# A two-layer hybrid decoder trunk: the first stage rebuilt with packed vectors, single-column modulation products and 28 instead of 16 filler products

## The chip, the cores and the metric

The kernel runs on one core of a Trainium2 chip. The metric is the device time of one execution in microseconds (us); lower is better. Three runs of the kernel before gave 257.09, 257.39 and 258.31 us, median 257.39.

The names of the engines: PE is TensorE (its matmuls), PEld its weight loads, DVE is VectorE, ACT is ScalarE, POOL is GpSimd, SP is SyncE, which issues nearly all DMAs.

## What is computed

The input x is 256 x 1024 (one batch), c is a conditioning vector of 1024. Two layers, each `x <- x + gate(c) * mixer(RMSNorm(x) * (1 + scale(c)) + shift(c))`. The first stage, which the change touches, is this part of the reference:

```python
cs = jax.nn.silu(c)
shift, scale, gate = jnp.split(cs @ mod_w[layer] + mod_b[layer], 3, axis=-1)
h = _modulate(_rmsnorm(x, norm_g[layer]), shift, scale)
...
u, g = jnp.split(h @ w_in, 2, axis=-1)
```

After it come a causal convolution of width 4, the RG-LRU gates and scan, an output projection, then shared keys and values, an attention layer with its own projections, and a last RMSNorm. All arrays are f32. The large products are done as three products each (`hi*hi`, `lo*hi`, `hi*lo`) of operands that are split into a rounded part `_hi` and a rest `_lo`.

## The kernel before

The 1024 features are 8 tiles of 128 (`KT`), the 256 positions 2 tiles (`ST`). All weights arrive in blocks of 512 KB, in the order of the string `ORDER`, over SP's queue, into 11 raw buffers (`NRAW`); a block's buffer is free again when its last reader is done. The host packs the blocks (`packed`, L105); it does not change a number.

Nothing is issued as it is written. Each operation is recorded (`Plan.record`, L154), and `Plan.order` (L362) sets an order for every engine with a table of costs, 80 random trials and priorities; the copies, the splits and the scalings (`plan.copy`, `plan.affine`, `plan.scale`) go to ACT or to DVE as it decides. The result is a fixed order on each engine: an instruction waits for all that stand ahead of it on its engine. Because one line issues all recorded operations, nearly every instruction has the line L409 (or L169, those that the planner gave an engine).

The first stage, by the names that the trace shows:

- SP loads c as 8 rows of 128, x in three pieces (`xr`), mod_b and norm_g as rows (`pa`), then the blocks. POOL loads seven more small vectors as rows (`pb`).
- PE runs filler products of `ones` (`warm`, L530: 16 there, and 4 in the bank `ga` ahead of the first real product). Each 128x128 f32 product is two records in the trace.
- silu(c) is made on the 8 rows, turned by a PE transpose (`pt_c`) and spread to 32 equal columns (`csB`); `pa` and `pb` are turned by PE too (`pt_a`, `pt_b`) and copied to `paT`, `pbT` by DVE.
- RMSNorm of x: squares and root on ACT (`sq_a`, `rv_a`), the rest on DVE (`rn`, `ry`, `rt`), the scaled rows `xn_a`, then 16 PE transposes (`tp_a`) and four copies to `xnT`.
- Shift and scale of layer 0: for the tiles 0 and 1 `mod_one` (L719), which is 16 products with 32 equal columns of csB as the stationary operand, four of them side by side in the array (`gvm0s`: 32 records), a copy (`partm0s`), one product with `sel2` that sums the four strips and turns the result (`mc_m0s`: 2 records) and two DVE operations (`sg4m0s`). The tiles 2 and 3 and the tiles 4 and 5 go in pairs with 256 columns (`mod_pair`, L642: `gvm`, `partm`, `mc_m`), the tiles 6 and 7 are summed on DVE (`mod_sum`).
- `mod_apply` (L725) makes `hrm`, `h_hi`, `h_lo` of a tile, and `u_rows` (L783) and `pair_T` (L506) do the three-part products `u` and `ga` with the split weights `wu`, `wga`. Each is one record a part.

Then `pj_wgc` (L498), the gates `pa` and `px` (L880), ACT's chain of exponentials and square roots, `r_wo`, a second RMSNorm (`rms("b...")`), `v`, `k`, and the attention layer.

Of the kernel before, what the change touches and what calls it, by code (L numbers as in the profile page):

```python
# [10 lines left out]
F32 = mybir.dt.float32  # L11
# [7 lines left out]
P = 128  # L19
# [6 lines left out]
NEG = -1e30  # L26
NRAW = 11
NSPL = 4
NWARM = 16
NWARM2 = 4  # L30
SUM0 = 3
LEAD = 2
CUT = 384

ORDER = """
    s0 wu0 s1 wu1 wga0 m01 wu2 wu3 m02 wga1 wu4 wu5 m03 wga2 wu6 wu7 wga3 wgc0 gax0 gax2 gax3 g0-0
    gax1 wgc1 g0-1 wo0 mk0 mk1 wo1 mk4 mk2 mk3 mk5 wv0 mk7 mk6 wv1 wv2 wv3 m10 wka0 wka1 wv4 wv5
    wka2 m12 wv6 m11 wv7 m13 m15 wka3 m14 wkb0 m16 m17 wkb1 wgb0 wgb1 wqa0 wgb2 wgb3 wqa1 wgb4 wgb5
    wqa2 wgb6 wgb7 wqa3 wqb0 wqb1 g1-0 wp0 wp1 g1-1
"""  # L40
# [7 lines left out]
def blocks():  # L48
# [4 lines left out]
    def want(name, shape, *src):  # L53
        out.append((name, shape, src))
# [8 lines left out]
    for b in ORDER.split():  # L63
        nm, i = b[:-1], int(b[-1])
        if nm == "s":
            for x, c0 in (("h", 0), ("c", D)):
                want(f"m0{x}0_{i}", (KT, P), ("mod_w", 0, 0, D, c0 + i * P, P))
        elif nm == "m0" and i >= SUM0:
            for q in range(4):
# [30 lines left out]


BLOCKS = blocks()


# [15 lines left out]
class Plan:  # L120
# [164 lines left out]


    def _forward(self, urge):
        ops, succ = self.ops, self.succ
# [11 lines left out]
        while len(seq) < n:  # L300
# [43 lines left out]
            for j in succ[i]:  # L344
                if ops[j]["pre"][i]:
                    at[j] = max(at[j], fin[i] + (950 if o["fn"] == "dma_start" else self._lat(o, ops[j])))
# [81 lines left out]
@with_exitstack  # L428
def kernel(ctx: ExitStack, tc: tile.TileContext, x, c, mod_b, norm_g, rg_conv_w, rg_conv_b,
                       rg_b_a, rg_b_x, rg_lambda, kv_norm_g, kv_mod_b, final_norm_g, pack, out):  # L430

# [14 lines left out]

    x, c, out = x[0], c[0], out[0]

# [11 lines left out]

    def split_into(raw, hi, lo):
        plan.copy(hi, raw)
        V.tensor_sub(lo, raw, hi.bitcast(F32))


    def wsplit(name):
        while len(halves) <= windex[name]:
            n = weights[len(halves)]
            t = got[n]
            shape = list(t.shape)  # L470
            hi = splp.tile(shape, F32R, tag="whi", name=n + "_hi", bufs=NSPL)
            lo = splp.tile(shape, F32R, tag="wlo", name=n + "_lo", bufs=NSPL)
            split_into(t, hi, lo)
            halves[n] = hi, lo
        return halves[name]
# [43 lines left out]
    pa = const.tile([64, P], F32, name="pa")  # L519
    SP.dma_start(pa[0:48], mod_b.rearrange("l (k p) -> (l k) p", p=P))  # L520
    SP.dma_start(pa[48:64], norm_g.rearrange("l (k p) -> (l k) p", p=P))
    load_all()
# [50 lines left out]

    def rms(nm, parts, early=None):
        bias, nbias = eps, neps
        for i, row in enumerate(parts):
            w = row.shape[-1]
            sq = tmp.tile([P, w], F32, tag="xn" if w > 512 else "tg", name=f"sq_{nm}{i}")
# [19 lines left out]

    def norm_T(row, rstd, xnT, s, nm):
        xn = tmp.tile([P, D], F32, tag="xn", name="xn_" + nm, bufs=2)  # L600
        plan.scale(xn, row, rstd)
        for q in range(2):
            ps = pbank(f"tp_{nm}{q}")
            for k in range(4):
                PE.transpose(ps[:, k * P:(k + 1) * P], xn[:, (4 * q + k) * P:(4 * q + k + 1) * P], ident)
            plan.copy(xnT[:, 4 * q:4 * q + 4, s * P:(s + 1) * P], ps.rearrange("p (k n) -> p k n", n=P))


# [19 lines left out]
    def mod_cols(tag, n, quads, gain, bias, pbank=pbank):  # L628
        gv = pbank(f"gv{tag}")
        gemv(gv, n * P, quads)  # L630
        part = tmp.tile([P, n * P], F32, tag="part", name=f"part{tag}", bufs=3)
        plan.copy(part, gv[:, 0:n * P])
# [85 lines left out]

    def mod_one(nm, i, k, gain, bias, pbank=pbank):  # L719
        ch = [got[f"{nm}{w}{i}_{k}"] for w in "hc"]  # L720
        quads = [[(csB[:, kt], ch[q // 2][:, kt]) for kt in range(q % 2, KT, 2)] for q in range(4)]
        m = 2 * i + k
        return mod_cols(f"{nm}s{m}", 1, quads, gain[:, m:m + 1], bias[:, m:m + 1], pbank)

# [29 lines left out]
    warm(NWARM, pbank("warm"))  # L754
    pt = bank("pt_a")
    PE.transpose(pt[:, 0:64], pa, ident[0:64, 0:64])
    paT = const.tile([P, 64], F32, name="paT")
    V.tensor_copy(paT, pt[:, 0:64])
    modbT = paT[:, 0:48].rearrange("p (l w k) -> p l w k", l=2, w=3)
# [11 lines left out]

    m0s = [mod_one("m0", 0, 0, *args0, bank)]
    for s in range(ST):
        norm_T(xr[:, s], rms(f"a{s}", [xr[:, s, 0:512], xr[:, s, 512:]] if s else [xr[:, s]], None if s else th[:, 0:1]), xnT, s, f"a{s}")
    m0s.append(mod_one("m0", 0, 1, *args0))

# [9 lines left out]

    for k in range(2):
        mod_apply("m0", k, 1, m0s[k], xnT, h0_h, h0_l)
        u_rows(k)
    nxt = mod_pair("m0", 1, *args0)  # L790
    pair_T(gb, "wga", h0_h, h0_l, 0)

    pt = pbank("pt_b")
    PE.transpose(pt[:, 0:88], pb, ident[0:88, 0:88])
    pbT = const.tile([P, 88], F32, name="pbT")
    V.tensor_copy(pbT, pt[:, 0:88])
    cwT = pbT[:, 0:32].rearrange("p (j k) -> p j k", j=4)
# [8 lines left out]


    nl = const.tile([P, KT], F32, name="nl")
    V.tensor_scalar(nl, lamT, -1.0, None, ALU.mult)
    na = const.tile([P, KT], F32, name="na")  # L810
    V.tensor_tensor(na, lamT, nl, ALU.min)
# [19 lines left out]

    for i in range(1, 4):
        mod_apply("m0", 2 * i, 2, nxt, xnT, h0_h, h0_l)
        if i < 3:
            nxt = (mod_pair if i + 1 < SUM0 else mod_sum)("m0", i + 1, *args0)
        for kt in (2 * i, 2 * i + 1):
            u_rows(kt)
        pair_T(gb, "wga", h0_h, h0_l, i)
# [247 lines left out]
    def fin(s, sl, b):  # L1086
# [26 lines left out]

_INS = ['x', 'c', 'mod_b', 'norm_g', 'rg_conv_w', 'rg_conv_b', 'rg_b_a', 'rg_b_x', 'rg_lambda',
        'kv_norm_g', 'kv_mod_b', 'final_norm_g', 'pack']
_OUTS = [((1, 256, 1024), 'float32')]
# [26 lines left out]
```

## Time and profile before

| | |
|---|---|
| median of three runs | 257.39 us (257.09 to 258.31) |
| the profiled execution | 257.7 us, of which 255.7 us from the first to the last instruction |
| PE busy | 242.2 us (95%), 1823 matmul records |
| weight loads (PEld) | 215.7 us (84%) |
| DVE, ACT, POOL busy | 208.8, 161.2, 18.3 us |
| DMA | 72.24 MB, mean 283 GB/s |
| granted TensorE clock | 0.992 of full speed (mean) |

The 2.0 us between 257.7 and 255.7 lie outside the instructions. "Busy" of PE says little here, since it is nearly always busy; what matters is when its first real product starts, what stands ahead of it, and in which stretches PE is the engine that ends last.

### The profile page before, as it was taken

What the parts mean: (1) busy time and instruction counts of PE and PEld (TensorE: products, weight loads), DVE (VectorE), ACT (ScalarE), POOL (GpSimd) and SP (SyncE); (2) the same over time, 40 slices, a digit from 0 to 9 for tenths busy, and PEclk for the clock granted to TensorE, in tenths of its full rate; (3) what the DMA queues carried; (4) which work ended last, traced back from release to release, by engine and by line L of the source; (5) the groups of instructions that cost most, each with busy time, mean ns of one, the idle gap of its engine ahead of it and who ended that gap; (6) DMA issues with size and microseconds to landing.
All of it is one profiled execution on the core that took longest, in us unless ns stands there. A gap on an engine that the chain in (4) does not pass through costs nothing.

```text
span 255.7 us, 4865 instructions
## 1 busy us (share of the span) xinstructions
PE 242.2 (95%) x1823; PEld 215.7 (84%) x1823; DVE 208.8 (82%) x378; ACT 161.2 (63%) x288; POOL 18.3 (7%) x31
## 2 busy tenths in 40 slices
PE   8899999999999996997999999999999999999970
PEld 7697799999897874865898898999999998889870
DVE  2773799899969999999898999973766789798483
ACT  7662755595799995079943385863537365786242
POOL 8100000000000033000000000010000000005030
PEclk9999999999999999999999999999999999999996
DMA  6999999992697879999999999986897520000003
GB/s 214 410 417 420 413 420 417 420 415 91 238 352 314 309 270 360 419 396 383 420 316 378 395 393 415 416 299 261 253 354 292 173 82 3 1 0 3 1 17 147
DMA packets 20695, 72.24 MB, mean 283 GB/s; under 512 B 2728, under 2 KB 3008, under 8 KB 20672
## 3 DMA queue, kind: packets, MB, share of 16 engines
q1 hardware_dynamic: 19840, 71.15, 71.9%
q0 software_dynamic: 688, 0.59, 0.9%
q8 instruction: 14, 0.23, 0.4%
q10 hardware_dynamic: 144, 0.20, 0.2%
q14 instruction: 9, 0.07, 0.1%
HBM read 70.87 MB, written 1.05 MB: 281 GB/s over the span
## 4 chain that ended last, share of the span: by engine, by line
PE 77%; ACT 12%; DVE 7%; issue 2%; DVEq 0%; ACTq 0%
PE u L409 9%; PE g L409 9%; PE v L409 9%; PE r_wp L409 6%; PE ga L409 5%; PE pj_wkb L409 5%; PE pj_wqb L409 5%; PE q L409 5%; PE k L409 4%; PE r_wo L409 3%; DVE x L409 3%; PE sc L409 3%; ACT L409 3%; PE warm L409 2%; PE pj_wgc L409 2%
## 5 line engine op out<-in xcount | busy, mean ns | idle before, releaser
L409 ACT ACT_TABLE_LOAD x14 | 18.0, 1283 | 1.0 <-PEq L1126 0.7
L409 PE MATMUL u<-h_lo,wu_hi 128*128 128x256 f32 x64 | 18.1, 285 | 0.0
L409 PE MATMUL u<-h_hi,wu_lo 128*128 128x256 f32 x64 | 18.1, 284 | 0.0
L409 PE MATMUL g<-h_hi,wgb_hi 128*128 128x256 f32 x64 | 18.0, 283 | 0.0
L409 PE MATMUL g<-h_lo,wgb_hi 128*128 128x256 f32 x64 | 18.0, 283 | 0.0
L409 PE MATMUL u<-h_hi,wu_hi 128*128 128x256 f32 x64 | 17.8, 288 | 0.0
L409 PE MATMUL g<-h_hi,wgb_lo 128*128 128x256 f32 x64 | 17.8, 283 | 0.0
L409 DVE SCALAR_TENSOR_TENSOR maccg<-g,csT,maccg 128x1024 f32<-128x1024 f32 x12 | 15.3, 1278 | 1.3 <-DMA g<-in_pack_dram 1.3
L409 POOL DMA_DIRECT2D row_g<-gsg x8 | 4.6, 582 | 142.1 <-issue 142.1
L409 PE MATMUL r_wp<-wp_hi,o_hi 128*128 128x512 f32 (+1 forms) x40 | 14.6, 364 | 0.0
L409 PE MATMUL r_wp<-wp_lo,o_hi 128*128 128x512 f32 (+1 forms) x40 | 14.2, 354 | 0.0
L409 PE MATMUL r_wo<-wo_hi,y_hi 128*128 128x512 f32 x32 | 12.4, 397 | 1.6 <-ACT y_hi L169 1.6
L409 PE MATMUL r_wp<-wp_hi,o_lo 128*128 128x512 f32 (+1 forms) x40 | 13.8, 350 | 0.0
L409 PE MATMUL v<-wv_hi,hk_hi 128*128 128x512 f32 x32 | 12.3, 394 | 1.3 <-ACT hk_hi L169 1.3
L409 PE MATMUL r_wo<-wo_hi,y_lo 128*128 128x512 f32 x32 | 12.3, 394 | 0.4 <-DVE y_lo L409 0.4
L409 DVE TENSOR_TENSOR wgb_lo<-wgb,wgb_hi 128x1024 fp32r<-128x1024 f32 x8 | 9.8, 1222 | 3.5 <-ACT wgb_hi L169 3.5
L409 PEld LDWEIGHTS u<-h_lo,wu_hi 128*128 128x128 f32 x64 | 12.2, 191 | 0.4 <-issue 0.4
L409 PEld LDWEIGHTS u<-h_hi,wu_lo 128*128 128x128 f32 x64 | 12.2, 191 | 0.4 <-issue 0.4
L409 PE MATMUL v<-wv_lo,hk_hi 128*128 128x512 f32 x32 | 12.5, 391 | 0.0
L169 ACT CAST wgb_hi<-wgb 128x1024 fp32r<-128x1024 f32 x8 | 8.4, 1048 | 6.3 <-PE g L409 3.7
L409 PE MATMUL r_wo<-wo_lo,y_hi 128*128 128x512 f32 x32 | 12.4, 397 | 0.0
L409 PEld LDWEIGHTS g<-h_hi,wgb_hi 128*128 128x128 f32 x64 | 12.3, 192 | 0.0
(306 smaller groups left out, 868.6 us busy)
## 6 DMA issues: line engine op xcount, KB each, us to landing
g<-in_pack_dram SPq DMA_DIRECT2D x16, 512.0 KB, 5.0
wu<-in_pack_dram SPq DMA_DIRECT2D x8, 512.0 KB, 10.0
wo<-in_pack_dram SPq DMA_DIRECT2D x8, 512.0 KB, 6.5
mkh<-in_pack_dram SPq DMA_DIRECT2D x8, 512.0 KB, 6.3
mkc<-in_pack_dram SPq DMA_DIRECT2D x8, 512.0 KB, 6.9
wv<-in_pack_dram SPq DMA_DIRECT2D x8, 512.0 KB, 7.3
m1h<-in_pack_dram SPq DMA_DIRECT2D x8, 512.0 KB, 5.2
m1c<-in_pack_dram SPq DMA_DIRECT2D x8, 512.0 KB, 5.3
```

The costliest lines, as they stand in the source:

```text
L169: self.record(eng, fn, args, kw, lambda f=f, args=args, kw=kw: f(*args, **kw))
L409: self.plan.record(self.name, fn, args, kw, lambda: f(*args, **kw))
```

## The change

- The host puts ten vectors into one array (`columns`): 160 columns of 128, loaded by one DMA of 128 x 160 f32 (80 KB) as `vT`. The ten small DMAs of c, `pa` and `pb` go (three on SP, seven on POOL), with the PE transposes `pt_c`, `pt_a`, `pt_b` and DVE's copies `paT`, `pbT`. x comes in two DMAs instead of three, and the squares of its second half in one piece.
- The first tile's shift and scale come from `mod_first`: 16 products with a 128x128 block of the modulation matrix as stationary operand and one column of csT moving, with no copy and no `sel2` product; one DVE and one ACT operation finish them.
- The first tile of h is made from the transposes in PSUM, not from `xnT`; its products run `hi*hi` for all 8 m first, then `lo*hi`, then `hi*lo`.
- The tiles 1, 2 and 3 each use `mod_one`; the pair of the tiles 2 and 3 goes.
- `NWARM` 16 to 28, `NRAW` 11 to 12 (the squares now write into a later tile's room), another `ORDER` of the blocks, and another guess of the planner at a DMA's time (`_far`).

```diff
-NRAW = 11
+NRAW = 12
...
-NWARM = 16
+NWARM = 28
...
-    s0 wu0 s1 wu1 wga0 m01 wu2 wu3 m02 wga1 wu4 wu5 m03 wga2 wu6 wu7 wga3 wgc0 gax0 gax2 gax3 g0-0
...
+    s0 wu0 s1 wu1 wga0 s2 s3 wu2 m02 wu3 wga1 wu4 wu5 wga2 m03 wu6 wu7
...
+VECTORS = ("c", "mod_b", "norm_g", "rg_conv_w", "rg_conv_b", "rg_b_a", "rg_b_x", "rg_lambda", "kv_norm_g", "kv_mod_b")
...
+def columns(inputs):
...
+    return np.concatenate([inputs[n].reshape(-1, P) for n in VECTORS]).astype(np.float32).T
...
-    c8 = const.tile([KT, P], F32, name="c8")
-    SP.dma_start(c8, c.rearrange("(k p) -> k p", p=P))
+    vT = const.tile([P, NV], F32, name="vT")
+    SP.dma_start(vT, vecs)
...
-    SP.dma_start(xr[:, 0], x[0:P])
-    for n in range(2):
-        SP.dma_start(xr[:, 1, n * 512:(n + 1) * 512], x[P:S, n * 512:(n + 1) * 512])
...
+    for s in range(ST):
+        SP.dma_start(xr[:, s], x[s * P:(s + 1) * P])
...
+    def mod_first(nm, m, gain, bias, both, new):
+        cp = new(f"mc_{nm}{m}")
+        for w in (1, 0):
+            t = got[f"{nm}{'hc'[w]}{m // 2}_{m % 2}"]
+            for kt in range(KT):
+                PE.matmul(cp[:, w:w + 1], t[:, kt], csT[:, kt:kt + 1], start=(w == 1 and kt == 0),
+                          stop=(w == 0 and kt == KT - 1), skip_group_check=True)
+        t4 = small.tile([P, 1, 2], F32, tag="sg2", name=f"sg2{nm}{m}", bufs=4)
+        V.tensor_scalar(t4[:, 0, 0:1], cp[:, 0:1], bias[:, m, 0:1], None, ALU.add)
+        A.activation(t4[:, 0, 1:2], cp[:, 1:2], AF.Identity, bias=both[:, m:m + 1], scale=gain[:, m:m + 1])
+        return t4
...
-    for k in range(2):
-        mod_apply("m0", k, 1, m0s[k], xnT, h0_h, h0_l)
-        u_rows(k)
-    nxt = mod_pair("m0", 1, *args0)
-    pair_T(gb, "wga", h0_h, h0_l, 0)
...
+    for s in range(ST):
+        sl = slice(s * P, (s + 1) * P)
+        A.activation(h0_h[:, 0, sl], tps[s][0][:, 0:P], AF.Identity, bias=t4[:, 0, 0:1], scale=t4[:, 0, 1:2])
+        V.tensor_scalar(hr[:, sl], tps[s][0][:, 0:P], t4[:, 0, 1:2], t4[:, 0, 0:1], ALU.mult, ALU.add)
+    V.tensor_sub(h0_l[:, 0], hr, h0_h[:, 0].bitcast(F32))
...
+    m0s.append(mod_one("m0", 1, *args0))
+    wh, wl = wsplit("wu_0", (first,))
+    for i, (w, h) in enumerate(((wh, h0_h), (wh, h0_l), (wl, h0_h))):
+        for m in range(KT):
+            PE.matmul(ub[m // 2][:, (m % 2) * S:(m % 2 + 1) * S], w[:, m * P:(m + 1) * P], h[:, 0],
+                      start=(i == 0 and m % 2 == 0), stop=False, skip_group_check=True)
...
+    for k in range(1, 4):
         mod_apply("m0", k, 1, m0s[k], xnT, h0_h, h0_l)
+        if k < 3:
+            m0s.append(mod_one("m0", k + 1, *args0))
+        else:
+            nxt = mod_pair("m0", 2, *args0)
         u_rows(k)
```

What this makes of the fixed orders is seen at three places. The first is PE from its start to its first real product (`u`). Before (the rows between are the rest of `gvm0s`, transposes, `mc_m0s` and fillers):

```order
L409 MATMUL warm<-ones 128x128 x6
L409 MATMUL pt_c<-ident,c_79 128x8
L409 MATMUL warm<-ones 128x128 x9
L409 MATMUL pt_a<-ident,pa 128x64
L409 MATMUL warm<-ones 128x128
L409 MATMUL tp_a_244<-ident,xn_a_243 128x128 x4
L409 MATMUL gvm0s_233<-m0h_0_83,csB 32x128 x2
...
L409 MATMUL ga_269<-ones 128x128 x3
L409 MATMUL gvm0s_258<-m0h_1_86,csB 32x128 x2
...
L409 MATMUL u_264<-h_hi,wu_hi 128x256
```

After:

```order
L426 MATMUL warm<-ones 128x128 x22
L426 MATMUL tp_a_235<-ident,xn_a_234 128x128 x4
L426 MATMUL tp_a_236<-ident,xn_a_234 128x128 x4
L426 MATMUL mc_m_246<-csT,m0c_0_82 128x1 x6
L426 MATMUL tp_a_243<-ident,xn_a_242 128x128 x4
L426 MATMUL tp_a_244<-ident,xn_a_242 128x128 x4
L426 MATMUL mc_m_246<-csT,m0c_0_82 128x1 x2
L426 MATMUL mc_m_246<-csT,m0h_0_83 128x1 x8
L426 MATMUL warm<-ones 128x128 x6
L426 MATMUL ga_255<-ones 128x128 x4
L426 MATMUL u_250<-h_hi,wu_hi 128x256 x2
```

Of the fillers, 22 now stand ahead of the first transposes and 10 between the last single-column product and the first `u`; the strips `gvm0s` of tile 1, which stood ahead of the first `u`, stand behind it.

The second place is PE right behind its first products. After (the next rows repeat the same strips of the same two blocks, and `u` with `h_lo`):

```order
L426 MATMUL u_250<-h_hi,wu_hi 128x256 x2
L426 MATMUL gvm0s_257<-m0h_1_86,csB 32x128 x2
L426 MATMUL gvm0s_257<-m0c_1_85,csB 32x128 x2
...
L426 MATMUL u_251<-h_hi,wu_hi 128x256 x2
L426 MATMUL u_252<-h_hi,wu_hi 128x256 x2
L426 MATMUL u_253<-h_hi,wu_hi 128x256 x2
L426 MATMUL mc_m0s_259<-sel_220,partm0s_258 128x2
L426 MATMUL u_250<-h_lo,wu_hi 128x256 x2
```

Three such groups of strips (tiles 1, 2, 3) now lie among the products of the stage, where before there was one of 256 columns (`gvm_276`, tiles 2 and 3).

The third is DVE on the way to the first scaled rows `xn_a`. Before:

```order
L409 RECIPROCAL ry_a_241<-rv_a_239 128x1
L409 COPY paT<-pt_a 128x64
L409 SCALAR_TENSOR_TENSOR rt_a_242<-ry_a_241,rn_a_240 128x1
L409 COPY pb_m_231<-paT 128x8
L409 COPY pb_m_232<-paT 128x8
L409 SCALAR_TENSOR_TENSOR ry_a_241<-rt_a_242,ry_a_241 128x1
L409 TENSOR_SCALAR rn_a_252<-ss_a_250,rb_a_248 128x1
L169 TENSOR_SCALAR xn_a_243<-xr,ry_a_241 128x1024
```

After:

```order
L426 TENSOR_SCALAR rn_a_231<-ss_a_229,neps 128x1
L426 RECIPROCAL ry_a_232<-rv_a_230 128x1
L426 SCALAR_TENSOR_TENSOR rt_a_233<-ry_a_232,rn_a_231 128x1
L426 SCALAR_TENSOR_TENSOR ry_a_232<-rt_a_233,ry_a_232 128x1
L426 TENSOR_SCALAR xn_a_234<-xr,ry_a_232 128x1024
```

The copy from `pt_a`, for which DVE waited on PE, no longer stands in between. Past the first stage the orders of ACT, DVE and PE hold the same operations in another sequence here and there.

## Rows read from the trace of the kernel before

**Rows 1.** The chain that ended last, in order of time: start us, us, what.

```profile
13.36 1.01 PE gvm0s L409 x32
14.37 0.90 PE u L409 x6
...
20.52 2.31 PE gvm L409 x32
...
23.74 0.34 PE mc_m L409 x4
...
55.70 5.76 PE pj_wgc L409 x48
...
68.41 0.84 ACT tx L409 x2
```

**Rows 2.** Busy by stretch: length, PE, PEld, DVE, ACT, POOL (instructions), clock, DMA, GB/s.

```profile
1.04:5.97 4.93, 4.93 (x21) 4.68 (x22) 1.67 (x10) 4.12 (x7) 4.67 (x11) 1.00 0.73 242
5.97:7.30 1.33, 1.32 (x11) 1.13 (x10) 0.42 (x4) 1.33 (x5) 1.04 (x2) 1.00 1.05 410
...
14.30:61.30 47.00, 47.00 (x424) 43.84 (x421) 38.47 (x82) 27.72 (x40) 0.00 (x0) 1.00 0.97 396
...
118.00:239.70 121.70, 121.70 (x874) 112.94 (x875) 99.63 (x155) 74.56 (x143) 4.39 (x6) 1.00 0.66 246
```

**Rows 3.** Fillers: timeline in two short windows (start, us); then shortest/median/longest ns.

```profile
2.48 1.27 PE L409 MATMUL warm<-ones 128*128 128x128 f32 x5
6.35 0.83 PE L409 MATMUL warm<-ones 128*128 128x128 f32 x6
...
L409 PE MATMUL warm<-ones x32: 275/421/582, 1.0 to 7.8; 128*128 128x128 f32 x32
```

**Rows 4.** Products of 2 columns and transposes: timelines, and shortest/median/longest ns.

```profile
23.46 0.54 PEld L409 LDWEIGHTS mc_m<-sel,partm 128*128 128x128 f32 x4
...
L409 PEld LDWEIGHTS mc_m<-sel,partm x8: 188/192/192, 23.5 to 32.2; 128*128 128x128 f32 x8
L409 PE MATMUL mc_m<-sel,partm x8: 168/251/251, 23.6 to 32.3; 128*128 128x2 f32 x8
...
11.41 0.28 PE L409 MATMUL mc_m0s<-sel,partm0s 128*128 128x2 f32 x2
...
9.11 0.66 PE L409 MATMUL tp_a<-ident,xn_a 128*128 128x128 f32 x4 [1.03 <-DVE xn_a L169]
```

**Rows 5.** Timelines of ACT and DVE: the way to the first transposes, and DVE's wait.

```profile
2.45 1.28 ACT L409 ACT_TABLE_LOAD   x1
...
4.59 1.06 ACT L409 ACTIVATE sq_a<-xr 128x1024 f32<-128x1024 f32 x1 [0.64 <-DMA xr<-in_x_dram]
...
6.39 0.28 ACT L409 ACTIVATE rv_a<-ss_a,eps 128x1 f32<-128x1 f32 x1
...
7.69 0.23 DVE L409 COPY paT<-pt_a 128x64 f32<-128x64 f32 x1 [0.77 <-PE pt_a L409]
...
8.30 0.75 DVE L169 TENSOR_SCALAR xn_a<-xr,ry_a 128x1024 f32<-128x1024 f32 x1
```

**Rows 6.** Timeline of ACT, 10.5 to 15.5: what makes the first tile.

```profile
12.63 0.60 ACT L169 ACTIVATE hrm<-xnT,sg4m0s 128x256 f32<-128x256 f32 x1
...
14.25 1.05 ACT L169 CAST wu_hi<-wu 128x1024 fp32r<-128x1024 f32 x1 [0.55 <-DMA wu<-in_pack_dram]
```

**Rows 7.** Timelines of POOL and DVE around 100, and of DVE near 115.

```profile
99.09 2.20 POOL L409 PARTITION_BROADCAST gate_g<-row_g  x1 [6.64 <-issue]
...
98.31 0.68 DVE L409 TENSOR_TENSOR y_lo<-sg,y_hi 128x512 fp32r<-128x512 f32 x1
...
100.04 1.65 DVE L409 TENSOR_TENSOR y_lo<-sg,y_hi 128x512 fp32r<-128x512 f32 x1
...
114.80 0.69 DVE L169 CAST wv_hi<-wv 128x1024 fp32r<-128x1024 f32 x1
```

**Rows 8.** DMA issue at 5.75 us: out<-in, KB, us to landing.

```profile
m0c<-in_pack_dram SPq DMA_DIRECT2D x1, 512.0 KB, 7.2
```

More of the change, by code (lines that the diff above doesn't have):

```diff
@@ L65, in blocks @@
         if nm == "s":
-            for x, c0 in (("h", 0), ("c", D)):
-                want(f"m0{x}0_{i}", (KT, P), ("mod_w", 0, 0, D, c0 + i * P, P))
-        elif nm == "m0" and i >= SUM0:
+            for x, c0 in (("c", D), ("h", 0)):
+                want(f"m0{x}{i // 2}_{i % 2}", (KT, P), ("mod_w", 0, 0, D, c0 + i * P, P))
+        elif b == "m03":
             for q in range(4):
@@ L284, in _tails, with _far @@
         return tail
+    @staticmethod
+    def _far(done):
+        return max(950, 2200 - 0.069 * (done - 6200)) if done > 6000 else 950
     def _forward(self, urge):
@@ L428, with kernel @@
 @with_exitstack
-def kernel(ctx: ExitStack, tc: tile.TileContext, x, c, mod_b, norm_g, rg_conv_w, rg_conv_b,
-                       rg_b_a, rg_b_x, rg_lambda, kv_norm_g, kv_mod_b, final_norm_g, pack, out):
+def kernel(ctx: ExitStack, tc: tile.TileContext, x, mod_b, final_norm_g, vecs, pack, out):
     nc = tc.nc
@@ L445 @@
     psp = plan.pool(ctx.enter_context(tc.tile_pool(name="psp", bufs=2, space=bass.MemoryType.PSUM)), 2)
[L447 removed]
+    x, out = x[0], out[0]
     weights = [b[0] for b in BLOCKS if b[0][0] == "w"]
@@ L458, in load_all, with split_into, wsplit @@
             SP.dma_start(t.rearrange("p k n -> p (k n)") if len(shape) == 2 else t, pack[i])
-    def split_into(raw, hi, lo):
+    def split_into(raw, hi, lo, after=()):
         plan.copy(hi, raw)
+        plan.after = after
         V.tensor_sub(lo, raw, hi.bitcast(F32))
-    def wsplit(name):
+        plan.after = ()
+    def wsplit(name, after=()):
         while len(halves) <= windex[name]:
@@ L472, in wsplit @@
             lo = splp.tile(shape, F32R, tag="wlo", name=n + "_lo", bufs=NSPL)
-            split_into(t, hi, lo)
+            split_into(t, hi, lo, after)
             halves[n] = hi, lo
@@ L597, in rms, with norm_T @@
         return y
-    def norm_T(row, rstd, xnT, s, nm):
+    def norm_T(row, rstd, xnT, s, nm, new=None):
         xn = tmp.tile([P, D], F32, tag="xn", name="xn_" + nm, bufs=2)
-        plan.scale(xn, row, rstd)
+        if new:
+            V.tensor_scalar(xn, row, rstd, None, ALU.mult)
+        else:
+            plan.scale(xn, row, rstd)
+        tps = []
         for q in range(2):
-            ps = pbank(f"tp_{nm}{q}")
+            ps = (new or pbank)(f"tp_{nm}{q}")
+            tps.append(ps)
             for k in range(4):
@@ L630, in mod_cols @@
         gemv(gv, n * P, quads)
-        part = tmp.tile([P, n * P], F32, tag="part", name=f"part{tag}", bufs=3)
+        part = tmp.tile([P, n * P], F32, tag="part", name=f"part{tag}", bufs=2)
         plan.copy(part, gv[:, 0:n * P])
@@ L754 @@
     warm(NWARM, pbank("warm"))
[L755 to L758, printed above, removed]
+    paT = vT[:, KT:KT + 64]
     modbT = paT[:, 0:48].rearrange("p (l w k) -> p l w k", l=2, w=3)
@@ L770 @@
     args1 = (normT[:, 1], pair_bias("m1", modbT[:, 1]))
[L772 to L775, printed above, removed]
+    tps = [norm_T(xr[:, s], rms(f"a{s}", [xr[:, s]], None if s else th[:, 0:1],
+                                     wg[:, 4 * s:4 * s + 4].rearrange("p k s -> p (k s)")), xnT, s, f"a{s}", bank)
+           for s in range(ST)]
+    both0 = const.tile([P, 1], F32, name="both0")
+    V.tensor_mul(both0, args0[0][:, 0:1], args0[1][:, 0, 1:2])
+    m0s = [mod_first("m0", 0, *args0, both0, bank)]
     h0_h = act.tile([P, KT, S], F32R, tag="hAh", name="h0_hi")
@@ L785, in u_rows @@
         gemm_T(ub, wh, wl, h0_h, h0_l, kt)
-    for k in range(2):
+    t4 = m0s[0]
+    hr = tmp.tile([P, S], F32, tag="hr", name="hr_first", bufs=3)
+    for s in range(ST):
[3 more added lines that the diff above has]
+    V.tensor_sub(h0_l[:, 0], hr, h0_h[:, 0].bitcast(F32))
+    first = len(plan.ops) - 1
+    m0s.append(mod_one("m0", 1, *args0))
[4 more added lines that the diff above has]
+                      start=(i == 0 and m % 2 == 0), stop=False, skip_group_check=True)
+    started = len(plan.ops) - 1
+    for k in range(1, 4):
         mod_apply("m0", k, 1, m0s[k], xnT, h0_h, h0_l)
+        if k < 3:
+            m0s.append(mod_one("m0", k + 1, *args0))
+        else:
+            nxt = mod_pair("m0", 2, *args0)
         u_rows(k)
-    nxt = mod_pair("m0", 1, *args0)
-    pair_T(gb, "wga", h0_h, h0_l, 0)
[L793 to L796, printed above, removed]
+        if k % 2:
+            pair_T(gb, "wga", h0_h, h0_l, k // 2)
+    pbT = vT[:, KT + 64:]
     cwT = pbT[:, 0:32].rearrange("p (j k) -> p j k", j=4)
@@ L805 @@
     argsk = (kvnT, pair_bias("mk", kvbT))
+    plan.after = (started,)
     nl = const.tile([P, KT], F32, name="nl")
     V.tensor_scalar(nl, lamT, -1.0, None, ALU.mult)
+    plan.after = ()
     na = const.tile([P, KT], F32, name="na")
@@ L830 @@
     V.tensor_scalar(n8, sp, -8.0, None, ALU.mult)
-    for i in range(1, 4):
+    for i in range(2, 4):
         mod_apply("m0", 2 * i, 2, nxt, xnT, h0_h, h0_l)
         if i < 3:
-            nxt = (mod_pair if i + 1 < SUM0 else mod_sum)("m0", i + 1, *args0)
+            nxt = mod_sum("m0", i + 1, *args0)
         for kt in (2 * i, 2 * i + 1):
@@ L1130 @@
     inputs["pack"] = packed(inputs)
+    inputs["vecs"] = columns(inputs)
     for name in _INS:
```

49 lines of the change are left out of this document (21 added, 28 removed).

## The prediction

> **What bounds the kernel now.** I read the chain that ended last first, then the busy time by stretch, then the timeline of the first 15 us. In the chain the reader should see one engine: from the strips `gvm0s` at 13.36 through the first real product at 14.37 to ACT's `tx` at 68.41 every piece shown is PE [rows 1]. The stretches say the same: between 14.30 and 61.30, where `pj_wgc` ends, PE is busy 47.00 of 47.00 us, though DMA runs at 396 GB/s beside it, and again 121.70 of 121.70 us later [rows 2]. In the first stretch only two things can move the end: when PE's first `u` starts, and how much work PE has from there to 61.30. What a vector, a copy or a transfer costs beside that is hidden until it holds up PE. From 68.41 ACT's chain takes over and passes a delay on, since it starts with the last gate products of PE.
>
> What holds the first `u` now is its place in PE's order. It stands behind the strips of tile 1, which take 1.01 us from 13.36 [rows 1] and need a block issued at 5.75 that takes 7.2 us to land, 12.95 [rows 8]. The change takes these strips out of the way. The question is what it puts there.
>
> **PE up to the first product.** Of the 28 fillers 22 now stand ahead of the first transposes; that is 44 records. They begin at 1.04 as before. The column of granted clock says 1.00 from the start, but the spacing does not: five fillers take 1.27 us, the last of them 421 ns, so (1.27 - 0.42) / 4 = 0.21 apart; later six take 0.83 with 275 ns for the last, (0.83 - 0.28) / 5 = 0.11 apart [rows 3]. That is a factor of two, the lower and the upper level of 1.2 and 2.4 GHz. The break is at 5.97: 21 records in the 4.93 us before it (a transpose and its wait among them), 11 in the 1.33 after [rows 2]. With nothing between them, 4.93 / 0.21 = 23 records fit ahead of 5.97; the other 21 take 21 x 0.11 = 2.3. The fillers end at about 8.3.
>
> Is x ready by then? ACT's second table load follows the tanh of c and ended at 3.73; the squares of x began at 4.59 when x had landed, 1.06, and the root took 0.28 [rows 5]. Now c comes inside an 80 KB transfer. Its landing lies between that of c alone and that of x right behind it in the queue, so the squares begin between 4.6 and 5.5. I take 4.7, nearer to c, since 80 KB is a sixth of x's first piece. Squares with their accumulator read some 1.25, root 0.28, three small DVE steps of some 0.2, then `xn_a` 0.75 [rows 5]: about 7.7. This is earlier than now, because DVE no longer waits 0.77 us for PE's `pt_a` [rows 5]. But it is ahead of the fillers' end, so it gains nothing: from 8.3 on PE's own queue counts. In it stand:
>
> - 16 transposes. Four take 0.66 [rows 4], less 0.27 for the length of the last, 0.13 apart, the first a little more: 8 take about 0.95, twice: 1.9.
> - 16 single-column products, each two records with a 128x128 f32 load of its own. No row shows one moving column. The nearest has two: the product with `sel2`. Four of its loads take 0.54 us, the last 0.19, so they are (0.54 - 0.19) / 3 = 0.117 apart [rows 4]. The lower end is what its moving columns alone cost: two such records take 0.28, the second 0.25 of it, so it starts 0.03 behind the first [rows 4]. I take 0.11, the spacing of the loads, because each of the 32 records needs another load. 32 x 0.11 = 3.55 (ends 1.0 and 3.7). The 32 strips of tile 0 that go cost 1.01.
> - 10 fillers: 20 records, 2.2.
>
> 8.3 + 1.9 + 3.55 + 2.2 = 16.0 for the first `u`, against 14.3: **+1.7**. Other limits lie below that. The two blocks of tile 0 are issued earlier and were there in time before. ACT must round the weights (1.05), finish the scale (some 0.3) and make two halves of `h_hi`, together somewhat over the 0.60 of `hrm` [rows 5, 6]. The rounding stands ahead of the end of the products at 13.8, the rest behind it: about 15.2. So the last fillers, not the data, set 16.0.
>
> **PE from there on.** The products `u`, `ga`, `pj_wgc` are the same in number. Out go the pair's strips, 2.31, and its four small records, 0.34 to 0.44 [rows 1, 4], and some 0.3 for tile 1's two records and `pt_b`. In come three groups of strips of 1.01 with two records of 0.11 each: 3 x 1.23 = 3.7. 3.7 - 3.05 = **+0.65** (up to 0.75). As PE has no idle time in this stretch [rows 2], all of it counts. The other order of the three parts, `hi*hi` first, hides waits for `lo`; there are none to save past 14.3.
>
> **What costs nothing.** The ten small DMAs and three transposes lay beside fillers. POOL's seven issues hold nobody. Twelve raw buffers and the new order of the blocks matter where PE waits for weights; in the 47.00 us it does so at most within the pair's 2.31. Squares of the second half in one piece end before PE wants them. Were PE's queue shorter, ACT's rounding of the weights would be late next.
>
> **After the first stage.** ACT's chain holds the same operations and as many table loads in a slightly other order; I count 0. Ahead of `v`, DVE no longer rounds a weight (0.69, [rows 7]) ahead of the columns that the next stage needs, while ACT has one more rounding between its squares: **-0.3** (0 to -0.5).
>
> Sum: 1.7 + 0.65 - 0.3 = +2.05, on the profiled execution's 257.7: 259.75. The median of the runs lies 0.3 below that execution, so I give **259.4**. With its own bounds this case runs from 258.6 (fillers ended at 7.7 by a clock that rises sooner, -0.6, and -0.5 ahead of `v`) to 260.4 (the clock rises 2 us later: in that time 9 records run instead of 18, and the 9 left over cost 1.0).
>
> **Rivals.**
>
> *Loads hidden, not slower.* If the single-column records follow each other by their moving column, at 0.03 us, they take 1.0 instead of 3.55, and PE would be ready for `u` at 13.5; the roundings and `h_hi` on ACT would then hold it to about 13.6. -0.7 + 0.65 - 0.3 = -0.35: 257.0. For it: the 0.03 between two records in rows 4. Against it: four loads in a row are 0.117 apart there. It decides at 0.05 us a record: 32 x (0.11 - 0.05) = 2 is all that the forecast loses. The Trainium skill, page "TensorE: Matmul & The Clock Gate", section "Back-to-back issue gap", gives some 25 ns for products of up to 64 moving columns; by it 32 records would be 0.8 us, an estimate from that page, and the sum would be this rival's 257.0. The loads of the `sel2` product do not agree with it.
>
> *A collision later on goes away, no change.* DVE's last `y_lo`, on the way to `r_wo`, takes 1.65 instead of 0.68 while POOL broadcasts the gate from 99.09 on, for 2.20 [rows 7]. The gate's sum stands elsewhere in DVE's order now. If the broadcast falls beside an idle DVE, 0.97 goes: 258.4. Against it: POOL started 6.64 us late for a reason that the trace does not show, and it can as well fall on another step of the same chain.
>
> *PE does not stay full, slower still.* The strips of three tiles each need a copy by ACT or DVE, a small product and two DVE steps ahead of the next tile, three times in a row, where before the pair had one for two tiles. If one of these chains comes 0.5 to 1 us late behind the long splits, or the clock rises later, 260.5. Against it: DVE is busy 38.47 and ACT 27.72 of 47.00 [rows 2].
>
> **How the numbers follow.** A run of this kernel can tell about 0.5% from no change, 1.3 us: 256.1 to 258.7. Forecast 0.6, loads hidden 0.1, collision gone 0.15, PE not full 0.15. Slower by more: nearly all of the forecast (0.57) and the last rival, 0.72. Within: the collision, the forecast's lower edge and half of the hidden loads, 0.23. Faster: the other half, where a second gain joins, 0.05. The range leaves out the hidden loads and the upper part of the last rival: 257.9 to 260.9.
>
> **What would show it.** First `u` near 16.0, with ten fillers right ahead of it and ACT's `h_hi` done before it; records of `mc_m` 0.11 apart; fillers ending near 8.3; `pj_wgc` ending near 63.6 with PE busy all the way from the first `u`. Wrong it is if `u` starts before 14.3, if the single-column records are closer than 0.05, or if the later stages take back more than 1 us.

## The result and the profile after

The changed kernel took 261.27 us, median of 20 runs (257.63 to 263.14), against 257.55 us before (257.09 to 258.39, 20 runs). The ratio is 1.0083, interval 1.0055 to 1.0112: slower, as forecast, and 1.0083 x 257.55 = 259.7 stands beside the forecast of 259.4. This ratio leaves out the six runs that lie more than 1.5% above the fastest one, but what sets them apart turned out to be the kernel's own doing, so the median of all runs, 1.4% up and 0.4 us above the forecast range, tells it better.

Why the runs of the changed kernel spread over 5 us where those of before spread over 1.3 is the main finding. Each run has a span and a mean granted clock of TensorE. With the 12 runs of a repetition below, 32 in all, there are three groups: nine with spans 255.9 to 256.8 at a clock of 0.989 to 0.995, six with 257.6 to 258.7 at 0.982 to 0.989, and 17 with 259.3 to 260.1 at 0.977 to 0.979. The profiled execution (263.14 us, span 260.1, clock 0.978) is one of the last. Its chain of waits in the first 22 us, which answers to [rows 1] (start us, us, what):

```profile
1.05 7.77 PE warm L426 x44
8.82 0.87 PE tp_a L426 x8
9.69 1.24 PE mc_m L426 x12
10.93 0.93 PE tp_a L426 x8
11.86 2.59 PE mc_m L426 x20
14.45 2.77 PE warm L426 x12
17.22 1.71 PE ga L426 x8
18.92 0.43 PE u L426 x2
19.35 1.42 PE gvm0s L426 x32
20.77 0.91 PE u L426 x6
```

The queue of TensorE alone leads to the first `u`, as forecast, but the pieces do not have one speed: 12 records of `mc_m` take 1.24 us and the next 20 take 2.59, 20 filler records (`warm` x12 and `ga` x8) take 4.48 where 20 at 0.11 would be 2.2. The busy time by stretch says why. Columns as in [rows 2]; the number ahead of the DMA share is the granted clock:

```profile
8.70:13.35 4.65, 4.65 (x46) 4.65 (x43) 0.56 (x1) 2.96 (x5) 0.00 (x0) 1.00 1.02 413
13.35:18.57 5.22, 5.22 (x26) 5.22 (x26) 2.60 (x5) 3.27 (x6) 0.00 (x0) 0.50 1.03 417
18.57:20.18 1.61, 1.61 (x24) 1.32 (x27) 0.00 (x0) 0.00 (x0) 0.00 (x0) 0.50 1.03 422
20.18:66.75 46.57, 46.57 (x469) 44.31 (x462) 36.70 (x78) 28.83 (x43) 0.00 (x0) 1.00 0.89 351
122.39:244.10 121.71, 121.71 (x873) 112.50 (x874) 101.00 (x154) 73.18 (x144) 4.21 (x6) 1.00 0.63 243
```

From 13.35 to 20.18 the granted clock is 0.50, 1.2 GHz instead of 2.4. What TensorE did before is the second thing to see: in the 4.65 us ahead it was busy for 4.65, with transposes and single-column products and nothing else. There was no idle gap. The line of the granted clock over the whole span, in 40 slices of 6.5 us, has the mark as its third digit:

```profile
PEclk9959999999999999999999999999999999999996
```

The last digit, 6, is no part of this: the kernel before has it too. TensorE's work is done by then, and the granted clock is 0.50 for the last 4.4 us here and the last 3.9 us before, which costs nothing but lowers a run's mean clock.

Half speed for 6.83 us loses 3.4, an estimate for a TensorE that is busy all the time. The first and the last group of runs lie 3.35 apart (middle of 259.3 to 260.1 against middle of 255.9 to 256.8). So the groups are probably runs without a fall, with a shorter one, and with this one. For the runs without a profile that is an inference from span and mean clock, and it is weakest between the first two groups: both have runs at 0.989, and no run of the middle group was profiled. The kernel before has a small second group as well: of the 77 runs of it beside the experiments below, 14 have spans of 255.9 to 256.7 at 0.986 to 0.987, where the others have 0.989 to 0.996. None of these 14 was profiled, so their cause stays open.

The products themselves, timeline of TensorE and instructions on the tile `mc_m` (shortest/median/longest ns), answer to [rows 4]:

```profile
9.53 1.40 PE L426 MATMUL mc_m<-csT,m0c 128*128 128x1 f32 x12
...
L426 PEld LDWEIGHTS mc_m<-csT,m0c x16: 190/192/192, 9.4 to 11.9; 128*128 128x128 f32 x16
L426 PE MATMUL mc_m<-csT,m0c x16: 169/250/250, 9.5 to 11.9; 128*128 128x1 f32 x16
```

Twelve records in 1.40 with a last one of 0.25: (1.40 - 0.25) / 11 = 0.105 apart, near the 0.117 of the loads in [rows 4] and far from 0.03. The fillers, timeline of TensorE in two short windows as in [rows 3]:

```profile
1.63 2.77 PE L426 MATMUL warm<-ones 128*128 128x128 f32 x12
...
6.76 1.95 PE L426 MATMUL warm<-ones 128*128 128x128 f32 x16
```

(2.77 - 0.42) / 11 = 0.21 apart early, (1.95 - 0.28) / 15 = 0.11 later, with a last one of 0.42 and 0.28: the two speeds that the forecast used.

From the first product on, the milestones of all kernels tell where time comes and goes. They are record starts in the one profiled execution of each (us). "Rise" is where the trace first records the clock at its upper level, and where the fillers' spacing goes from 0.21 to 0.11 (the views print 1.00 ahead of it as well). "Half clock again" is the stretch at 0.50 behind that, the end of the span left out. e0 to e9 are the runs of the next section:

```
kernel              rise  half clock again  first u  first pj_wgc  first v   span
before               6.1  no                 14.30      55.53      117.98   255.7
changed              6.5  13.35 to 20.18     18.57      60.90      122.39   260.1
e0 changed, again    5.6  12.43 to 19.25     18.57      60.45      121.91   259.4
e1 128 columns       7.1  no                 16.42      57.99      119.43   257.2
e2 and no late       4.5  no                 14.90      56.54      117.98   255.5
e3 strips            4.5  no                 14.48      56.44      117.88   255.6
e4 f32 products      6.0  16.28 to 19.69     19.05      60.95      122.41   259.9
e5 no late           5.8  12.62 to 19.44     16.09      59.22      120.67   258.2
e6 strips, s2        7.1  no                 15.46      56.60      118.05   255.6
e7 and 18            6.6  no                 14.73      55.82      117.26   254.9
e8 and only 18       6.7  no                 14.79      56.34      117.78   255.4
e9 128, s2, only 18  4.7  no                 14.94      56.51      118.00   255.5
```

The changed kernel is 4.27 us late at the first `u`, 5.37 at `pj_wgc`, 4.41 at `v`, 4.4 at the end. From `pj_wgc` to `v` it takes 61.49 where before took 62.45, and this is 61.44 to 61.49 in all eleven variants whatever their first stage did. So about 1.0 us is a gain in that stage of the new order itself, not slack that takes up a delay: e7 reaches `pj_wgc` within 0.3 us of the kernel before and has the gain all the same.

### The profile page after: what moved, and what is told of

Same layout as the page of the kernel before. It is cut to its first block, busy times and chain, and to the rows that moved or that the text cites. A ratio compares the mean times of both kernels' runs of the same rounds, so it can differ in the third digit from the quotient of the medians.

```text
span 260.1 us, 4945 instructions
## 1 busy us (share of the span) xinstructions
PE 248.8 (96%) x1874; PEld 224.0 (86%) x1874; DVE 208.7 (80%) x372; ACT 162.0 (62%) x293; POOL 13.8 (5%) x24
## 3 DMA queue, kind: packets, MB, share of 16 engines
HBM read 70.87 MB, written 1.05 MB: 276 GB/s over the span
## 4 chain that ended last, share of the span: by engine, by line
PE 82%; ACT 7%; DVE 6%; issue 2%; DMA 1%; DVEq 0%; ACTq 0%
PE u L426 9%; PE g L426 9%; PE v L426 9%; PE r_wp L426 8%; PE ga L426 5%; PE pj_wkb L426 4%; PE r_wo L426 4%; PE pj_wqb L426 4%; PE k L426 4%; PE q L426 4%; PE warm L426 4%; PE sc L426 3%; DVE x L426 2%; PE pj_wgc L426 2%; PE oT L426 2%
## 5 line engine op out<-in xcount | busy, mean ns | idle before, releaser
L426 PE MATMUL u<-h_hi,wu_hi 128*128 128x256 f32 x64 | 17.1, 296 | 0.0
L426 PE MATMUL u<-h_lo,wu_hi 128*128 128x256 f32 x64 | 16.8, 284 | 0.0
L426 PE MATMUL u<-h_hi,wu_lo 128*128 128x256 f32 x64 | 16.8, 284 | 0.0
L181 ACT CAST wgb_hi<-wgb 128x1024 fp32r<-128x1024 f32 x7 | 7.4, 1053 | 9.3 <-PE g L426 3.6
L181 ACT CAST wv_hi<-wv 128x1024 fp32r<-128x1024 f32 x7 | 7.4, 1051 | 8.4 <-PE r_wo L426 4.0
L426 PE MATMUL v<-wv_hi,hk_lo 128*128 128x512 f32 x32 | 12.5, 394 | 0.0
L426 PEld LDWEIGHTS u<-h_hi,wu_hi 128*128 128x128 f32 x64 | 11.5, 193 | 1.0 <-issue 1.0
L426 DVE TENSOR_TENSOR wp_lo<-wp,wp_hi 128x1024 fp32r<-128x1024 f32 x8 | 9.7, 1218 | 3.3 <-ACT wp_hi L181 3.2
```

Of the source, the lines that this page charges most:

```text
L181: self.record(eng, fn, args, kw, lambda f=f, args=args, kw=kw: f(*args, **kw))
L426: self.plan.record(self.name, fn, args, kw, lambda: f(*args, **kw))
```

## The experiments

The theory after the result: transposes and single-column products, though they fill TensorE's time, do not hold its clock, and what comes behind them (ten late fillers, the first `u`, the strips of tile 1) then runs at half speed. The rivals: the cost is the queue alone, at one speed, as the forecast had it; or the clock falls for a reason that has nothing to do with what TensorE does there.

**e0, the changed kernel again.** No edit.

> The changed kernel as it is, for a second profile and more times. Clock theory: its runs fall into the same groups by mean granted clock as before, 0.995 with spans near 256.0, 0.988 to 0.990 with 256.4 to 258.7, 0.977 to 0.979 with 259.3 to 260.1, median near 261.3 us; in the profile the granted clock falls to half near 13.4 us or later, at the end of the transposes and single-column products, or not at all in a run of the first group. Rival, a fall that has nothing to do with what TensorE does there: the same groups, but the fall stands at another time in this profile.

Measured: 261.48 us (258.10 to 262.07, 12 runs), before 257.37 (31 runs), ratio 1.0117 (1.0083 to 1.0151). The groups came again, 3, 2 and 7 runs. The fall stands at 12.43, again inside the single-column products, though 0.9 us earlier than the "near 13.4 us or later" that was expected; the rise was 0.9 us earlier too. By itself this run does not decide between the theory and the last rival; e1 does.

**e1, 128 equal moving columns.** The vector is broadcast along the moving side; the readers take columns 0 and 128, and the planner keeps its old price, so that order and number of records stay.

```diff
-                PE.matmul(cp[:, w:w + 1], t[:, kt], csT[:, kt:kt + 1], start=(w == 1 and kt == 0),
+                PE.matmul(cp[:, w * P:(w + 1) * P], t[:, kt], csT[:, kt:kt + 1].broadcast_to([P, P]), start=(w == 1 and kt == 0),
                           stop=(w == 0 and kt == KT - 1), skip_group_check=True)
+                plan.ops[-1]["cost"] = 109
...
-        A.activation(t4[:, 0, 1:2], cp[:, 1:2], AF.Identity, bias=both[:, m:m + 1], scale=gain[:, m:m + 1])
+        A.activation(t4[:, 0, 1:2], cp[:, P:P + 1], AF.Identity, bias=both[:, m:m + 1], scale=gain[:, m:m + 1])
```

> Same order and same number of instructions; the 16 single-column products of the first tile have 128 equal moving columns instead of one, all else is as in the changed kernel. Clock theory (transposes and single-column products do not hold the clock): granted clock 1.0 from about 6.5 us to the end in every run, the ten late fillers take 2.2 us instead of 4.5, first u near 16.1 to 16.4 instead of 18.6, one group of times, median 257.7 to 258.5 us. Rival, the queue alone (records of 0.11 us each set by their weight load): nothing changes, records still 0.11 apart, median 261.3 and the same groups. Rival, a fall that has nothing to do with what TensorE does: median 261.3 and the same groups.

Measured: 258.62 us (257.91 to 258.99, 8 runs), ratio to before 1.0040 (1.0027 to 1.0054), all clocks 0.990 to 0.994: one group. Its chain of waits from the transposes on:

```profile
9.11 0.87 PE tp_a L426 x8
9.98 1.34 PE mc_m L426 x12
11.32 0.87 PE tp_a L426 x8
12.20 2.23 PE mc_m L426 x20
14.43 1.34 PE warm L426 x12
15.77 0.89 PE ga L426 x8
16.66 0.24 PE u L426 x2
16.90 1.01 PE gvm0s L426 x32
```

The stretches from the transposes to the first `u` have the clock at 1.00:

```profile
8.95:14.40 5.45, 5.45 (x52) 5.45 (x51) 0.36 (x1) 3.09 (x5) 0.00 (x0) 1.00 1.02 416
14.40:16.42 2.02, 2.02 (x21) 2.02 (x20) 1.34 (x4) 1.66 (x4) 0.00 (x0) 1.00 1.02 416
```

127 more columns per product cost nothing in the queue (20 records take 2.23, 0.11 each, the spacing that single-column records have at the upper clock), and 2.9 us of median went: the late fillers take 2.23 instead of 4.48, the strips 1.01 instead of 1.42. The median is 0.1 above the range that the clock theory gave, and 2.6 below the 261.3 that both rivals wanted from the same records in the same order. The moving columns, and with them the columns written, were the only thing changed, and the fall went.

**e2, the same without the ten late fillers.** The program's own order is kept and fillers past the 22nd are skipped when it is written out.

```diff
+            idle = 0
             for i in self.order():
-                self.ops[i]["call"]()
+                idle += self.ops[i]["idle"]
+                if not self.ops[i]["idle"] or idle <= 22:
+                    self.ops[i]["call"]()
```

> As the one with 128 moving columns, and the ten late fillers between the last single-column product and the first u left out. Clock theory: granted clock stays 1.0, first u near 15.5, set by the halves of h_hi on ScalarE, about 0.7 us earlier than with the fillers: median near 257.0 to 257.8. If the 1.6 us in which TensorE then waits let the clock fall, it is 259 or more. Queue theory: first u at 15.5 to 16.1, median near 260.7.

Measured: 257.79 us (257.23 to 258.27, 12 runs), ratio 1.0010 (0.9997 to 1.0022). The gain of 0.83 is the expected one, and a wait of 1.6 us ahead of `u` did not let the clock fall. The first `u`, 14.90, is earlier than expected because in this execution the clock had risen at 4.5 and the first 22 fillers were done by 7.85.

**e3, strips for the first tile**, as before the change, planned anew.

```diff
-    both0 = const.tile([P, 1], F32, name="both0")
-    V.tensor_mul(both0, args0[0][:, 0:1], args0[1][:, 0, 1:2])
-    m0s = [mod_first("m0", 0, *args0, both0, bank)]
+    m0s = [mod_one("m0", 0, *args0)]
```

> The first tile's shift and scale made by 32-column strips and a product with sel2, as in the kernel before, all else as in the changed kernel and planned anew by its planner, which puts the strips of tile 1 ahead of the first u again. Sum from the rows: fillers end 8.66, then 16 transposes 1.9, two groups of strips 2.0, ten fillers 2.2 and the small product 0.2, first u near 15.0, and 1.0 less work behind it. Clock theory: clock 1.0 throughout, median 255.5 to 257. Queue theory: 2.4 below the changed kernel's median, 258.9. A fall that has nothing to do with what TensorE does: 258.9 with groups.

Measured: 257.32 us (256.81 to 258.29, 12 runs), ratio 0.9996 (0.9984 to 1.0008). The clock stayed up, and the whole loss of the change is gone with this one part and the order that the planner then made, but the further gain that was expected did not come. The chain of waits shows what took it: a transfer.

```profile
8.26 11.07 DMA m0h<-in_pack_dram
19.32 0.14 issue
19.46 1.08 PE gvm0s L426 x32
```

The first `u` is at 14.48, but TensorE then sat 0.84 us idle for tile 2, whose block landed at 19.3. Everything else in the change (one array for the vectors, 12 raw buffers, the other order of blocks and of the parts of `u`) is still in this kernel, and its sum is nothing that shows: 0.91 us late at `pj_wgc`, most of it that wait, and 1.0 back by `v`. What each of these parts is worth alone was not tried.

**e4, the transposes as ordinary products**, single columns as in the change.

```diff
-                PE.transpose(ps[:, k * P:(k + 1) * P], xn[:, (4 * q + k) * P:(4 * q + k + 1) * P], ident)
+                o, i = ps[:, k * P:(k + 1) * P], xn[:, (4 * q + k) * P:(4 * q + k + 1) * P]
+                if new:
+                    PE.matmul(o, i, ident, start=True, stop=True, skip_group_check=True)
+                    plan.ops[-1]["cost"] = 107
+                else:
+                    PE.transpose(o, i, ident)
```

> The 16 transposes of x made as ordinary f32 products with the identity of 128 moving columns (two records each), the single-column products of the first tile as in the changed kernel, same order. TensorE has 16 records more, 1.8 us at 0.11. If the single-column products alone let the clock fall: the granted clock falls to half at their end in most runs as in the changed kernel, groups of times, median near 263.2. If the transposes are needed for the fall as well: clock 1.0 throughout, one group, near 260.4 (the one with 128 moving columns, 258.6, plus 1.8). A fall that has nothing to do with what TensorE does is excluded already.

Measured: 261.10 us (259.54 to 261.92, 6 runs), ratio 1.0128 (1.0098 to 1.0157). It lies between the two answers. Four runs have a mean clock of 0.983 to 0.985, two have 0.992 and the two lowest times. Stretches of its profile:

```profile
8.59:16.28 7.69, 7.69 (x71) 7.69 (x71) 0.71 (x2) 3.64 (x6) 0.00 (x0) 1.00 1.03 416
16.28:19.69 3.41, 3.41 (x18) 3.24 (x16) 2.38 (x4) 2.79 (x4) 0.00 (x0) 0.50 1.02 419
19.69:25.00 5.31, 5.31 (x80) 4.92 (x83) 3.33 (x8) 2.29 (x3) 0.00 (x0) 1.00 1.03 420
```

The single-column products can bring the fall without transposes, but here it lasts 3.41 us, half of that in the changed kernel, and by their mean clock two runs go without. The transposes have their part: with them the fall is longer, 6.83 us in the two profiles of the changed kernel. Whether it is also more frequent can't be told: four of six runs here against 23 of the 32 in the two upper groups there. (In e1 the transposes without single columns brought none.) The records of `tp_a`, twice as many, take 3.68 instead of 1.80, and the shorter fall gave about as much back. The Trainium skill, page "TensorE: Matmul & The Clock Gate", section "Part 4: PE-mode transpose", says that transposes don't count as TensorE's activity in the way that products do; these profiles agree: 6.83 us at half clock with them, 3.41 with products in their place.

**e5, no late fillers, single columns as in the change.** The edit of e2 on the changed kernel.

> Single-column products as in the changed kernel, only the ten late fillers left out. Clock theory: the fall stays in most runs; in those TensorE's first u comes near 16.1 instead of 18.6, but its first products run at half clock for longer, so of the 2.5 us about half is left, median 260 to 260.7, lowest runs near 257.3; if TensorE's wait of 1.6 us keeps the clock low beyond 20.2 us, 261 or more. Queue theory, late fillers cost their whole length: 2.5 below the changed kernel, 259.

Measured: 260.03 us (258.57 to 260.93, 6 runs), ratio 1.0095 (1.0070 to 1.0120). The first `u` comes 2.5 us earlier, and 1.45 of the median is left of it, as the clock theory has it. Stretches:

```profile
8.47:12.60 4.13, 4.13 (x41) 4.13 (x39) 0.67 (x1) 2.56 (x5) 0.00 (x0) 1.00 1.01 410
12.60:19.40 6.80, 5.17 (x47) 4.37 (x47) 2.89 (x6) 3.88 (x6) 0.00 (x0) 0.50 1.03 418
19.40:25.00 5.60, 5.60 (x71) 5.27 (x70) 4.04 (x13) 3.82 (x6) 0.00 (x0) 1.00 1.03 421
```

The half clock is there without the late fillers, for the same time, and takes the first products instead of them. So the ten late fillers neither brought the fall nor prevented it. The lowest run missed the expected 257.3 by 1.3; with six runs, whose mean clocks are 0.977 to 0.987, it may be that none was without a fall.

**e6, e7, e8, e9: is there a version that beats both?** In all four, the blocks of tile 2 are loaded ahead of those of `wga0`. e6 is e3 with that alone. e7 is e6 with 18 fillers ahead of the transposes instead of 22, e8 has these 18 and no other (the last condition is only `idle <= 18`; the late fillers left out are 10, not the 13 of its expectation), and e9 is e1 with the other order of the blocks, the same 18 and no other.

```diff
-    s0 wu0 s1 wu1 wga0 s2 s3 wu2 m02 wu3 wga1 wu4 wu5 wga2 m03 wu6 wu7
+    s0 wu0 s1 wu1 s2 wga0 s3 wu2 m02 wu3 wga1 wu4 wu5 wga2 m03 wu6 wu7
...
+            idle = 0
             for i in self.order():
-                self.ops[i]["call"]()
+                idle += self.ops[i]["idle"]
+                if not self.ops[i]["idle"] or idle <= 18 or idle > 22:
+                    self.ops[i]["call"]()
```

> As the one with strips for the first tile, and the two blocks of tile 2 loaded ahead of the two of wga0. There TensorE waited 0.84 us for tile 2, which landed at 19.3; now it should land 2.6 us earlier and the wait go. If that passes on to the end: 256.5. If the wait for the transfer of mkh, to 101.9, sets the middle of the kernel: 257.3, no change. If wga0 is late instead: 257.3 to 258.

> The same with 18 instead of 22 fillers ahead of the first transposes. In the profiles so far the clock rose at between 4.5 and 7.1 us and the 22 fillers ended at 7.85 to 9.1, while xn_a is there at 7.6. With 18 they end at 7.0 to 8.2: 0 to 0.9 earlier first transposes, on the mean 0.4, so 256.1 to 257.2 by whether the first stage reaches the end. If the short wait ahead of the transposes lets the clock fall: 258 or more.

> As the last one, and the 13 fillers between the transposes and the first u left out too. TensorE then waits for x, for the columns of the first tile and for tile 1, which landed at 13.6: some 3 to 4 us without work ahead of 13.6, then 1.0 of strips, first u near 14.7 if the clock stays up: 256.2 to 257.1, no more than in the run with fillers. If the waits let the clock fall, the strips and the first products run at half speed: 1 to 3 us more, 258 to 260, and the granted clock shows it.

> The products with 128 moving columns for the first tile, tile 2 loaded earlier, 18 early fillers and no other: fillers end 7.0 to 8.2, 1.9 and 3.55 behind it, h_hi 1.6 later, first u 14.4 to 15.2, strips of tile 1 behind it. If the clock stays up: against the one with 128 columns and without late fillers (257.79) 0.4 to 0.9 less, 256.9 to 257.4; the same as with strips, so that products with the weights as the stationary side would be no gain at any clock. If the waits let it fall: 259 or more.

Measured: e6 257.01 us (256.52 to 257.87), ratio 0.9977 (0.9963 to 0.9990); e7 257.12 (256.02 to 257.76), 0.9982 (0.9969 to 0.9994); e8 257.52 (256.12 to 257.88), 0.9991 (0.9976 to 1.0007); e9 257.36 (257.01 to 258.05), 0.9989 (0.9976 to 1.0002); 12 runs each. The wait for tile 2 went in e6, and 0.3 of the 0.8 reached the median; where the rest went was not found. e6 and e7 are 0.2% faster than the kernel before, which is too little to matter. Four fillers fewer made no difference that shows. e8 missed its expectation, 256.2 to 257.1. Its chain of waits lies on transfers from the start, to 30.08:

```profile
2.10 6.06 DMA m0c<-in_pack_dram
...
8.18 10.24 DMA wga<-in_pack_dram
...
18.49 11.59 DMA wu<-in_pack_dram
```

But these transfers do not explain the miss: the first `u` is at 14.79, as expected, and from there to `pj_wgc` TensorE is idle for 0.1 us of 41.55. Its profile shows no fall of the clock. The mean clocks of five of its runs are 0.982 to 0.988, though, where no run of e3, e6, e7 and e9 is below 0.989, so some may have had one; that stays open. e9 came as expected, and as fast as the kernel before: with 128 moving columns and the clock held, products with the weights on the stationary side are an even trade against strips in this place, and no gain.

## Why the prediction was right, and where not

The sign and, by the ratio, the size came out. The reasons did so in part only, and the size came out by luck: the runs lie in groups on both sides of the forecast 259.4, the middle of the lowest near 258.4 and of the highest near 261.7, and the ratio is taken over the mixture of them, without the six slowest.

**Right:** TensorE's own queue sets the first `u`; nothing else does. `h_hi` was there at 16.03 in the changed kernel's execution, well ahead of 18.57. It is the end of this row of ACT:

```profile
15.12 0.91 ACT L426 ACTIVATE h_hi<-tp_a,sg2m 128x128 fp32r<-128x128 f32 x2
```

The single-column records follow each other at 0.11 while the clock is up, and not at 0.03: the rival with the hidden loads fell. (The Trainium skill, page "TensorE: Matmul & The Clock Gate", section "Back-to-back issue gap", gives its 25 ns for products by themselves, and says that in a stream of weight loads and products both set the spacing; this trace, with a load for each record and 0.11, agrees with the second.) Transposes: 0.87 + 0.93 = 1.80 for 1.9. The small edits cost nothing in sum, as e3 shows. `xn_a` was ready at 7.81, forecast 7.7, ahead of the fillers' end. These readings by rows of the nearest kind held.

**Wrong, the step that failed:** "from 8.3 on PE's own queue counts", with every record of it at 0.11. That the clock stays at its upper level after its first rise was taken for granted, since before the change it did; the text asked only when it would rise. By the chain, the terms up to the first `u` are: fillers' end 8.82 for 8.3, transposes 1.80 for 1.9, single columns 3.83 for 3.55, ten late fillers 4.48 for 2.2. Of the 2.9 us by which the sum missed this execution's chain (18.92 for 16.0), 2.3 lie in the late fillers alone, which the fall to 0.50 at 13.35 made twice as long. The forecast's rival "PE does not stay full, slower still" named a late rise and starved products, and its 260.5 lies near the measured median, but its mechanism is not what happened: TensorE was full throughout.

**Mis-sized:** the strips, +0.65. From the first `u` to `pj_wgc` e1, which keeps its clock, takes 41.57 against 41.23 before: +0.34. The changed kernel has 42.33, and the excess over e1 of 0.76 is what half speed until 20.18 costs there. The later stages, -0.3 (0 to -0.5): measured -1.0 from `pj_wgc` to `v`. The last `r_wo` ends at 110.47 before and 115.38 after, `v` starts at 117.98 and 122.39. So the stretch ahead of `v` that the forecast priced gave 0.50, the far end of its range, and the stretch between `pj_wgc` and the end of `r_wo` another 0.46 that the forecast had as 0. Together they stay just short of the 1 us that the forecast named as a sign of being wrong. Which of the moved operations gives this was not tried.

**The sum corrected.** With the clock held (e1): +2.1 at `u`, +0.3 by `pj_wgc`, -1.0 by `v`, +1.4 to +1.5; the medians say 258.62 - 257.37 = +1.25. With the fall of 6.83 us: 3 us more. The two errors of the forecast, no fall (too low by up to 3) and a later gain put too small (too high by 0.7), partly cancel in the mean over runs. So a number near the ratio came out, and that is the luck of it.

**The rival of the collision** did not come true. POOL's broadcast, which [rows 7] had on `y_lo`, still meets DVE, only on another instruction. Timelines of POOL and of DVE (start us, us):

```profile
101.97 1.58 POOL L426 PARTITION_BROADCAST gate_g<-row_g  x1 [5.83 <-issue]
...
102.30 1.66 DVE L426 TENSOR_TENSOR_SCAN aq<-aq,wgx 128x256 f32<-128x256 f32 x1
...
104.60 0.69 DVE L426 TENSOR_TENSOR y_lo<-sg,y_hi 128x512 fp32r<-128x512 f32 x1
...
106.33 0.69 DVE L426 TENSOR_TENSOR y_lo<-sg,y_hi 128x512 fp32r<-128x512 f32 x1
```

Both `y_lo` take 0.69 now, and the last of the scans, 0.68 in the kernel before, takes the 1.66. So the rival's own objection, that the broadcast can fall on another step of the same chain, is what happened.

## What to carry to other kernels

A TensorE that is busy all the time can still lose its clock: where a stretch is made of transposes and products with one moving column, look at the granted clock of the stretch behind it, and price what stands there at both levels. Where each product has a weight load of its own, as here, try more moving columns: 128 instead of 1 cost no time in these runs and kept the clock, which was worth 2.9 us of median for one broadcast operand. When a kernel's times spread in groups, read the span and the mean clock of each run before any average, and remember that the idle end of a run is in that mean too.

## What the runs showed of the hardware that was not expected

- The granted clock fell to half with no idle gap on TensorE ahead of it: behind 4.65 us of transposes and single-column products, all of them busy. With 128 moving columns and the same records it stayed up, by the profile of one run and the mean clocks of all eight (0.990 to 0.994). A wait of 1.6 us (in the profiles of e2 and e9) did not bring it down.
- An f32 product of 128x128 weights takes 0.11 us a record with 1 moving column as with 128, at the upper level of the clock and with a weight load for each record.
- The first rise of the clock came between 4.5 and 7.1 us from the start in eleven executions (all but that of the kernel before) whose TensorE does the same fillers, 18 or 22, from 1.05 on. The first transposes behind 22 fillers start anywhere from 7.76 (e2) to 8.95 (e1) by that, so where fillers stand on the path, the first stage has over a microsecond of play from execution to execution.
